# Attention scores, maxima and values by double steps, with TensorE's order as written

## The chip, the cores and the metric

The kernel runs on one core of a Trainium2 chip, in one launch. The core has five engines that this document names by the profile's short names: PE (TensorE, the matrix unit; PEld is its loading of weights), DVE (VectorE), ACT (ScalarE), POOL (GpSimd) and SP (SyncE, which issues the DMAs). Each runs its own list of instructions in order, and they wait for each other through semaphores. The metric is the time of one execution on the device in microseconds; the median of several executions is given.

## The reference, cut to what matters

Two layers on 512 latent tokens with a prefix of 256 context tokens, width 1024: an attention layer and a Mamba-2 layer, each followed by a gated feed-forward part. The change touches the attention layer alone:

```python
def gqa_attend(q, k, v):
    s = jnp.einsum('bqhgd,bkhd->bhgqk', q, k).astype(jnp.float32) * (HEAD_DIM ** -0.5)
    p = jax.nn.softmax(s, axis=-1).astype(v.dtype)
    return jnp.einsum('bhgqk,bkhd->bqhgd', p, v)

def attention_mixer(h_lat, h_ctx, w_qkv, q_norm, k_norm, w_o, need_ctx_out):
    q_l, k_l, v_l = jnp.split(h_lat @ w_qkv, [Q_DIM, Q_DIM + KV_DIM], axis=-1)
    ...
    k_all = jnp.concatenate([k_l, k_c], axis=1)
    v_all = jnp.concatenate([v_l, v_c], axis=1)
    ...
    o_l = ob.transpose(1, 0, 2, 3, 4, 5).reshape(bsz, seq, Q_DIM) @ w_o
    ...
        o_c = gqa_attend(q_c, k_c, v_c).reshape(bsz, l_ctx, Q_DIM) @ w_o
    return o_l, o_c
```

There are 16 query heads of 64 columns and 4 key heads. Latent queries attend to 768 keys, context queries to the 256 context keys. Queries and keys are normed and rotated first.

## The kernel before, in words

**Pairs and steps.** Heads are worked on two at a time: eight pairs (`Pair`), one head in partitions 0 to 63 and the other in 64 to 127. A pair has seven steps (`steps`, from L790). Steps 0 to 5 take one block of 128 keys each against all 512 latent queries; step 6 takes the two context blocks against the 256 context queries. A step is

- the **scores** (L835, L837): four pairs of matmuls into a PSUM tile `ps_s` of 1024 columns, three for the product in split precision and one that adds the negated row maxima (`diag`); 64 rows of the array for each head, so that the two run side by side ("64\*128" in the profile);
- the exponential (L838) on ACT into a tile `pr`, of which there are three;
- the sum over key blocks (L843, L845, L849) on DVE into `acc`.

What follows a step runs one step later (`later_lat`, `later_ctx`): the **values** (L799), matmuls of `pr` with the values of that key block into the PSUM bank `ps_o` or, for context, `ps_oc` ("128\*64"). After the last latent block and after the context blocks `final` closes the softmax: matmuls with ones over `acc` (L805, `ps_sum` or `ps_oc`), logarithm and exponential on ACT (L808, L809), three operations on DVE (L810 to L812).

**Maxima.** Row maxima of pair p + 1 are found while pair p runs (`maxima`, from L751): seven units, each of one or two scores in plain precision into a PSUM tile `ps_m` (L761, also "64\*128") and a reduction on DVE (L765). The last unit makes `diag` from them (L781, L786), so that the next pair's first scores need it.

**Buffers.** `ps_s` and `ps_m` share two PSUM tiles of two banks each (tag "S"). All else in PSUM shares four single banks (tag "B"): `ps_o`, `ps_sum`, `ps_oc`, the norms' `ssq`, and the filler's `ps_q`, `ps_ada`, `ps_adt`, `ps_d`.

**Filler.** Between steps a planner (`Weave`) puts other work on PE: projections of the later pairs' queries (`ps_q`), the modulation (`ps_ada`, `ps_adt`), and the output projection of finished pairs (`ps_d`), all but `ps_ada` with the whole array ("128\*128"). It divides what is left evenly over the 56 steps. "Lights" are small pieces with a due step and a condition, at most one a step: the chains that norm and rotate queries (`queries`, whose `ssq` matmuls are "64\*64"), splits of weights, splits of finished outputs (`osplit`). Lights that a pair's maxima need are run at the latest before these.

**The order on PE.** The loop (L965 to L992) emits, in each step: scores, a unit of maxima, the last step's values, filler. In the last step of a pair the maxima come before the scores. The framework's scheduler then orders the instructions of each engine. It follows the emitted order by priority, but moves instructions forward where its own model says that an earlier one isn't ready. An earlier part of attention, the first projections, pins PE, ACT and DVE to the emitted order (`manual_schedule`, L524 to L637); the steps don't.

**After the steps** the last pair's output is split (`osplit(7)`), and the projection of the last three pairs follows (`ps_dn`), then the feed-forward part.

Of the kernel before, what the change touches and what calls it, by code (L numbers as in the profile page):

```python
# [17 lines left out]
L = 512  # L18
# [3 lines left out]
NH = 16  # L22
# [489 lines left out]
def attention(g, adas, project, X):  # L512
# [4 lines left out]
    Bk, Sb = (lambda name: Bank(g, name)), (lambda name: S(g, name))  # L517
# [5 lines left out]
    ET = mybir.EngineType  # L523
# [220 lines left out]
    class Pair:  # L744
# [45 lines left out]
        def steps(self):  # L790

            (qh, ql), (kh, kl) = qprep[self.p], k2[self.kv]
            po = acc = None
            o = g.t3p.tile([P, T], F32, tag="o", bufs=2, name=f"o{self.p}")

            def values(po, pr, t, off, n, first, last):
                v = vt[t][:, self.kv * HD : (self.kv + 1) * HD]
                for e in range(2):
                    nc.tensor.matmul(po[S64[e], :n], v, pr[:, 512 * e + off : 512 * e + off + n], start=first, stop=last)  # L799

            def final(po, ps, acc, out):

                n = out.shape[-1]
                for e in range(2):
                    nc.tensor.matmul(ps[S64[e], :n], g.ones[:, :HD], acc[:, n * e : n * e + n], start=True, stop=True)  # L805
                y, u = t2("y")[:, :n], t2("u")[:, :n]

                nc.scalar.activation(y, ps, AF.Ln)  # L808
                nc.scalar.activation(y, y, AF.Exp, scale=-1.0)  # L809
                nc.vector.tensor_tensor(out, po, y, ALU.mult)  # L810
                nc.vector.scalar_tensor_tensor(u, ps, -1.0, y, ALU.mult, ALU.mult)
                nc.vector.scalar_tensor_tensor(out, u, 2.0, out, ALU.add, ALU.mult)  # L812

            def later_lat(po, pr, t, acc):
                values(po, pr, t, 0, L, t == 0, t == 5)
                if t == 5:
                    final(po, Bk("ps_sum"), acc, o[:, :L])

            def later_ctx(pr, acc):
                pc = Bk("ps_oc")  # L820
# [7 lines left out]
            for t in range(7):  # L828
                ps, pr = Sb("ps_s"), g.t3p.tile([P, 1024], F32, tag="pr", bufs=3, name="pr")
                for q0, n, k0, off in (((0, L, t * P, 0),) if t < 6 else ((L, C, L, 0), (L, C, L + P, C))):  # L830
                    q, k = slice(q0, q0 + n), slice(k0, k0 + P)
                    outs = [ps[:, 512 * e + off : 512 * e + off + n] for e in range(2)]
                    for i, (a, b) in enumerate(((kh, qh), (kl, qh), (kh, ql))):
                        for e in range(2):
                            nc.tensor.matmul(outs[e], a[S64[e], k], b[S64[e], q], start=i == 0, stop=False)  # L835
                    for e in range(2):
                        nc.tensor.matmul(outs[e], onesr[S64[e]], self.diag[S64[e], q], start=False, stop=True)  # L837
                nc.scalar.activation(pr, ps, AF.Exp)  # L838
                if t == 0:
                    po = Bk("ps_o")  # L840
                elif t == 1:
                    acc = g.t3p.tile([P, 1024], F32, tag="acc", bufs=1, name="acc")
                    nc.vector.tensor_tensor(acc, prev, pr, ALU.add)  # L843
                elif t < 6:
                    nc.vector.tensor_tensor(acc, acc, pr, ALU.add)  # L845
                else:
                    acc = t2("accc")
                    halves = pr.rearrange("p (e k q) -> p e k q", e=2, k=2)
                    nc.vector.tensor_tensor(acc.rearrange("p (e q) -> p e q", e=2), halves[:, :, 0], halves[:, :, 1], ALU.add)  # L849
                prev = pr  # L850
                yield (lambda t=t, pr=pr, po=po, acc=acc: later_lat(po, pr, t, acc)) if t < 6 else (
                    lambda pr=pr, acc=acc: later_ctx(pr, acc))
            g.o.append(o)

# [107 lines left out]
        pass  # L962
    for _ in qfirst:
        pass
    late_step = None  # L965
    for p in range(NH // 2):
        m = iter(())
        if p < 7:
            for it in [it for it in weave.lights if it in {2: q2, 3: q3}.get(p + 1, qc.get(p + 1, [])) + (kk if p == 3 else [])]:
                it.run()  # L970
                weave.lights.remove(it)
            m = pairs[p + 1].maxima()
        own = pairs[p].steps()
        for t in range(7):
            if t == 6:
                next(m, None)
            todo = next(own)
            if t < 6:
                next(m, None)
            if late_step:  # L980
                late_step()
            late_step = todo
            for it in list(free):
                if it.at <= weave.now and it.ready(weave.now):
                    it.run()
                    it.when = weave.now
                    free.remove(it)
            weave.step()
            if p == 7 and t == 3:
                osplit(6)  # L990
        next(own, None)
    late_step()  # L992
    assert not weave.lights, len(weave.lights)
    weave.drain()
    osplit(7)


# [722 lines left out]
```

## Time and profile before

| | us |
|---|---|
| median of 3 runs | 1887.12 (1885.73 to 1887.31) |
| span of the profiled execution | 1884.5 |
| first scores start | 111.14 |
| last projection (`ps_dn`) starts | 375.26 |
| busy from 111 to 376, of 265: PE, DVE, ACT | 259.61, 225.88, 130.11 |

The profiled execution has no time of its own beside its span; the span runs from the first to the last instruction of the program, and the median of the runs lies 2.6 us above it. In the profile's lines L835 is line 835 of the kernel; "out<-in" gives the tiles written and read; "64\*128 64x512" is the shape of the array that a matmul uses and its moving operand; "x8" counts instructions. A line of the timeline begins with the start and the duration in us, and "[0.60 <-DVE qsq]" is idle time of the engine before it and what ended it. A matmul's duration includes its way through the array, so that the next may start before it ends. A line of the waits gives the waiting engine, tile and line, whom it waited for, and in us the total, the number and the longest.

### The profile page before, as it was taken

To read this page: it belongs to the slowest core of one execution; us is meant where nothing else is said; L and a number is where in the kernel's file an instruction comes from. 1 tells how busy PE (TensorE), PEld (TensorE's weight loads), DVE (VectorE), ACT (ScalarE), POOL (GpSimd) and SP (SyncE) were. 2 spreads that over 40 slices of the span, in tenths; PEclk is the share of its full clock that TensorE was granted. 3 is DMA by queue.
4 is the path that set the end of the run, shared out by engine and by line. 5 is a ranking of instruction groups with operands and counts; after the bars stand their busy time and mean duration, and the time that the engine had idled before them with its cause. 6 is when DMAs were issued, how large, how long until landed. Compare 5 with 4: busy or idle time off the path is not lost.

```text
span 1884.5 us, 27447 instructions
## 1 busy us (share of the span) xinstructions
PE 1860.0 (99%) x10794; PEld 1531.3 (81%) x10794; DVE 1348.8 (72%) x2013; ACT 832.6 (44%) x1422; POOL 232.5 (12%) x220
## 2 busy tenths in 40 slices
PE   9999999999999999999999999999999999999999
PEld 7865545689888888888888888888887888888887
DVE  5688999678877777444478977777888676565655
ACT  3655544354222222222257577766667352323331
POOL 2100000030000000000031243443334200000000
PEclk9999999999999999999999999999999999999999
DMA  9223241015444554222224243434344323323332
GB/s 342 70 82 118 84 145 62 18 50 189 136 134 124 176 180 146 68 68 67 67 79 140 70 121 114 133 113 135 120 126 125 100 78 101 101 87 104 90 101 90
DMA packets 73489, 210.02 MB, mean 111 GB/s; under 512 B 8976, under 2 KB 14480, under 8 KB 73232
## 3 DMA queue, kind: packets, MB, share of 16 engines
q1 hardware_dynamic: 73360, 208.26, 35.2%
q8 instruction: 85, 1.39, 0.3%
q14 instruction: 44, 0.36, 0.1%
HBM read 198.79 MB, written 6.82 MB: 109 GB/s over the span
## 4 chain that ended last, share of the span: by engine, by line
PE 80%; DVE 10%; issue 4%; ACT 3%; DMA 2%; POOL 1%; SPq 0%; DVEq 0%; POOLq 0%; ACTq 0%
PE ps_up L105 10%; PE ps_up L106 10%; PE ps_up L108 10%; PE ps_d L105 6%; PE ps_d L108 6%; PE ps_d L106 5%; PE ps_in L105 4%; PE ps_in L108 4%; PE ps_in L106 3%; PE ps_o L799 2%; PE ps_s L835 2%; PE ps_st L1340 1%; DVE wl L87 1%; DVE xf L1212 1%; PE ps_wo L106 1%
## 5 line engine op out<-in xcount | busy, mean ns | idle before, releaser
L87 DVE TENSOR_TENSOR wl<-wst,wh 128x1024 fp32r<-128x1024 f32 x211 | 261.0, 1237 | 246.5 <-PE ps_up L106 125.4
L85 ACT CAST wh<-wst 128x1024 fp32r<-128x1024 f32 x211 | 220.8, 1048 | 413.5 <-DMA wst<-in_wup 316.2
L106 PE MATMUL ps_up<-hlf,wh 128*128 128x512 f32 x992 | 351.6, 354 | 0.0
L108 PE MATMUL ps_up<-hhf,wl 128*128 128x512 f32 x992 | 351.4, 354 | 0.0
L105 PE MATMUL ps_up<-hhf,wh 128*128 128x512 f32 x992 | 351.2, 355 | 0.0
L105 PEld LDWEIGHTS ps_up<-hhf,wh 128*128 128x128 f32 x992 | 187.5, 189 | 26.2
L106 PEld LDWEIGHTS ps_up<-hlf,wh 128*128 128x128 f32 x992 | 187.6, 189 | 26.0
L108 PEld LDWEIGHTS ps_up<-hhf,wl 128*128 128x128 f32 x992 | 187.5, 189 | 26.1
L105 PE MATMUL ps_in<-hhs,wh 128*128 128x512 f32 (+1 forms) x544 | 199.7, 367 | 0.0
L108 PE MATMUL ps_in<-hhs,wl 128*128 128x512 f32 (+1 forms) x544 | 193.5, 356 | 0.0
L106 PE MATMUL ps_in<-hls,wh 128*128 128x512 f32 (+1 forms) x544 | 193.3, 355 | 0.0
L108 PE MATMUL ps_d<-hdh,wl 128*128 128x512 f32 (+1 forms) x496 | 173.4, 350 | 0.0
L105 PE MATMUL ps_d<-hdh,wh 128*128 128x512 f32 (+1 forms) x496 | 173.3, 350 | 0.1
L106 PE MATMUL ps_d<-hdl,wh 128*128 128x512 f32 (+1 forms) x496 | 172.9, 349 | 0.0
L1022 DVE SCALAR_TENSOR_TENSOR X<-ps_d,mod,X 128x256 f32<-128x256 f32 (+1 forms) x176 | 102.7, 614 | 27.1 <-PE ps_d L108 27.0
L105 PEld LDWEIGHTS ps_in<-hhs,wh 128*128 128x128 f32 x544 | 102.8, 189 | 15.5 <-issue 1.9
L108 PEld LDWEIGHTS ps_in<-hhs,wl 128*128 128x128 f32 x544 | 102.7, 189 | 15.0
L106 PEld LDWEIGHTS ps_in<-hls,wh 128*128 128x128 f32 x544 | 102.9, 189 | 13.0
L106 PEld LDWEIGHTS ps_d<-hdl,wh 128*128 128x128 f32 x496 | 93.2, 188 | 14.4 <-DVE hdl L87 0.2
L108 PEld LDWEIGHTS ps_d<-hdh,wl 128*128 128x128 f32 x496 | 93.2, 188 | 13.1
L105 PEld LDWEIGHTS ps_d<-hdh,wh 128*128 128x128 f32 x496 | 93.0, 188 | 13.0 <-ACT hdh L85 0.3
L168 DVE SCALAR_TENSOR_TENSOR junk<-wada,cb 128x1024 f32<-128x1024 f32 x80 | 97.5, 1218 | 1.1 <-ACT cb L159 0.8
(375 smaller groups left out, 3632.9 us busy)
## 6 DMA issues: line engine op xcount, KB each, us to landing
wst<-in_wup SPq DMA_DIRECT2D x88, 512.0 KB, 3.5
wada<-in_adaT SPq DMA_DIRECT2D x56, 512.0 KB, 3.8
wst<-in_win SPq DMA_DIRECT2D x48, 512.0 KB, 3.6
wst<-in_wdown SPq DMA_DIRECT2D x44, 512.0 KB, 3.7
E<-ad SPq DMA_DIRECT2D x64, 256.0 KB, 6.7
wada<-in_adaB SPq DMA_DIRECT2D x24, 512.0 KB, 4.6
ec<-ead SPq DMA_DIRECT2D x64, 128.0 KB, 4.6
wst<-in_wout SPq DMA_DIRECT2D x16, 512.0 KB, 3.7
```

Source lines behind the costliest of these rows:

```text
L85: keep(nc.scalar.copy(hi, src))
L87: keep(eng.tensor_tensor(lo, src, _r(hi), ALU.subtract))
L105: mm(out, wh, ah, start=first, stop=False)
L106: mm(out, wh, al, start=False, stop=False)
L108: i = mm(out, wl, ah, start=False, stop=last)
L168: g.tc.keep_in_program_order(nc.vector.scalar_tensor_tensor(junk, w, 1.0, cb[:, v * D : (v + 1) * D], ALU.mult, ALU.mult, accum_out=md[:, ...
L799: nc.tensor.matmul(po[S64[e], :n], v, pr[:, 512 * e + off : 512 * e + off + n], start=first, stop=last)
L835: nc.tensor.matmul(outs[e], a[S64[e], k], b[S64[e], q], start=i == 0, stop=False)
L1022: nc.vector.scalar_tensor_tensor(ap, o[:, c0:c1], gate[:, m, v : v + 1], ap, ALU.mult, ALU.add)
L1212: i = nc.vector.scalar_tensor_tensor(cv, raw[:, tap : tap + n], par(f"sw{tap}", j), cv, ALU.mult, ALU.add)
L1340: nc.tensor.matmul(ps[:, d * 256 : (d + 1) * 256], Bt[:, t * P : (t + 1) * P], xw[d][t], start=t == ts[0], stop=t == ts[-1])
```

## The change

The loop takes the 56 steps two at a time, across the borders of pairs: 28 double steps. Each emits the scores of both steps, then the values (and closings) of the two steps before, then two units of maxima, then two portions of filler. The maxima of pairs 1 to 7 are one stream, drawn two units a double step after one unit ahead of the loop; the lights that a pair needs are run when the stream reaches it. PE keeps the emitted order over the whole loop and the drain of what is left (`manual_schedule` for PE); ACT, DVE and the rest stay with the scheduler. The bank `ps_o` is taken at the first values instead of the first scores. The split of pair 6's output is emitted before the late values of its double step. After the loop the last two steps' values and closings follow each other.

```diff
@@ steps @@
-            po = acc = None
+            po, acc = [], None
...
-            def later_lat(po, pr, t, acc):
-                values(po, pr, t, 0, L, t == 0, t == 5)
+            def later_lat(pr, t, acc):
+                if t == 0:
+                    po.append(Bk("ps_o"))
+                values(po[0], pr, t, 0, L, t == 0, t == 5)
                 if t == 5:
-                    final(po, Bk("ps_sum"), acc, o[:, :L])
+                    final(po[0], Bk("ps_sum"), acc, o[:, :L])
...
-                if t == 0:
-                    po = Bk("ps_o")
-                elif t == 1:
+                if t == 1:
...
@@ the loop @@
-    late_step = None
-    for p in range(NH // 2):
-        m = iter(())
-        if p < 7:
-            for it in [it for it in weave.lights if it in {2: q2, 3: q3}.get(p + 1, qc.get(p + 1, [])) + (kk if p == 3 else [])]:
+    def stream():
+
+        for p in range(1, NH // 2):
+            for it in [it for it in weave.lights if it in {2: q2, 3: q3}.get(p, qc.get(p, [])) + (kk if p == 4 else [])]:
                 it.run()
                 weave.lights.remove(it)
-            m = pairs[p + 1].maxima()
-        own = pairs[p].steps()
-        for t in range(7):
+            yield from pairs[p].maxima()
+
+    m, own, late = stream(), None, []
+    man = g.tc.manual_schedule(engines={ET.PE})
+    man.__enter__()
+    next(m)
+    for d in range(7 * NH // 4):
+        todo = []
+        for p, t in (divmod(2 * d, 7), divmod(2 * d + 1, 7)):
+            if t == 0:
+                own = pairs[p].steps()
+            todo.append(next(own))
             if t == 6:
-                next(m, None)
-            todo = next(own)
-            if t < 6:
-                next(m, None)
-            if late_step:
-                late_step()
-            late_step = todo
+                next(own, None)
+            if p == 7 and t == 4:
+                osplit(6)
+        for f in late:
+            f()
+        late = todo
+        for _ in range(2):
+            next(m, None)
+        for _ in range(2):
             for it in list(free):
                 if it.at <= weave.now and it.ready(weave.now):
                     it.run()
                     it.when = weave.now
                     free.remove(it)
             weave.step()
-            if p == 7 and t == 3:
-                osplit(6)
-        next(own, None)
-    late_step()
+    for f in late:
+        f()
     assert not weave.lights, len(weave.lights)
     weave.drain()
+    man.__exit__(None, None, None)
     osplit(7)
```

More of the change, by code (lines that the diff above doesn't have):

```diff
@@ L838, in steps @@
                 nc.scalar.activation(pr, ps, AF.Exp)
-                if t == 0:
-                    po = Bk("ps_o")
-                elif t == 1:
+                if t == 1:
                     acc = g.t3p.tile([P, 1024], F32, tag="acc", bufs=1, name="acc")
                     nc.vector.tensor_tensor(acc, prev, pr, ALU.add)
-                elif t < 6:
+                elif 0 < t < 6:
                     nc.vector.tensor_tensor(acc, acc, pr, ALU.add)
-                else:
+                elif t:
                     acc = t2("accc")
@@ L850, in steps @@
                 prev = pr
-                yield (lambda t=t, pr=pr, po=po, acc=acc: later_lat(po, pr, t, acc)) if t < 6 else (
+                yield (lambda t=t, pr=pr, acc=acc: later_lat(pr, t, acc)) if t < 6 else (
                     lambda pr=pr, acc=acc: later_ctx(pr, acc))
```

## The prediction

> **What bounds the kernel now.** The page comes first, for the engine that sets the end.
>
> ```profile
> span 1884.5 us, 27447 instructions
> PE 1860.0 (99%) x10794; PEld 1531.3 (81%) x10794; DVE 1348.8 (72%) x2013; ACT 832.6 (44%) x1422; POOL 232.5 (12%) x220
> PE 80%; DVE 10%; issue 4%; ACT 3%; DMA 2%; POOL 1%; SPq 0%; DVEq 0%; POOLq 0%; ACTq 0%
> ```
>
> The chain that ended last runs on PE for 80% of the span. A busy PE is not a PE at its peak, so I count from the starts of its matmuls. The change touches one stage only, from the first scores (111.1 us) to the output projection (375.3 us). Second view, the table of stretches: the stage, its middle, and the stretch in which DVE is fullest.
>
> ```profile
> 111.00:376.00 265.00, 259.61 (x1612) 148.43 (x1611) 225.88 (x324) 130.11 (x174) 0.00 (x0) 1.00 0.27 87
> 145.00:340.00 195.00, 190.53 (x1184) 107.69 (x1182) 175.54 (x249) 97.09 (x130) 0.00 (x0) 1.00 0.30 98
> 185.00:225.00 40.00, 37.45 (x241) 21.60 (x240) 36.78 (x50) 20.54 (x27) 0.00 (x0) 1.00 0.33 104
> ```
>
> After the stretch and its length stand PE, PE's weight loads, DVE and ACT. PE is nearly always in a matmul, but DVE is busy 175.54/195 = 0.90 of the middle and 36.78/40 = 0.92 of the fullest part. It is the second bound, close behind.
>
> Third view, PE alone in order of time: a single step, values with their closing sums, and a filler of nine matmuls.
>
> ```profile
> 185.84 0.49 PE L835 MATMUL ps_s<-qh,kh 64*128 64x512 f32 x2
> ...
> 186.63 0.39 PE L837 MATMUL ps_s<-diag,onesr 64*128 64x512 f32 x2
> 186.86 0.40 PE L761 MATMUL ps_m<-kh,qh 64*128 64x512 f32 x2
> 187.19 1.08 PE L799 MATMUL ps_o<-pr,v 128*64 128x512 f32 x4
> ...
> 173.00 1.08 PE L799 MATMUL ps_o<-pr,v 128*64 128x512 f32 x4
> 173.91 1.03 PE L805 MATMUL ps_sum<-acc,ones 128*64 128x512 f32 x4
> 174.87 0.64 PE L129 MATMUL ps_ada<-wada,sc 128*32 128x512 f32 x4
> ...
> 351.75 1.08 PE L799 MATMUL ps_o<-pr,v 128*64 128x512 f32 x4
> 352.76 0.50 PE L105 MATMUL ps_d<-hhol,wh 128*128 128x512 f32 x1
> ...
> 355.02 0.50 PE L835 MATMUL ps_s<-qh,kh 64*128 64x512 f32 x2
> ```
>
> Inside a run of one array shape (the pair of numbers behind the operands), pairs of score matmuls start 0.23 us apart (186.63 to 186.86). The run of four score pairs and a pair of maxima, all 64\*128, takes 187.19 - 185.84 = 1.35 us, though five times 0.23 is 1.15: **a run costs 0.20 us beyond its matmuls**. Values, 128\*64: alone 352.76 - 351.75 = 1.01; with as many closing matmuls 174.87 - 173.00 = 1.87; so four cost 0.86 and the run 0.15. Filler, 128\*128: nine take 355.02 - 352.76 = 2.26 against 9 x 0.23 = 2.07, so 0.2. A change of shape is what doubling steps saves.
>
> **The change part by part.** *Runs saved.* Two single steps are now six runs (scores with maxima, values, filler, twice): 2 x (0.20 + 0.15 + 0.20) = 1.10 us. A double step is four (scores, values, maxima, filler): 0.75. In the first 24 of 28 double steps that saves 0.35 each, 8.4 us. The last four have no maxima left and three runs: 0.55 saved each, 2.2 us. Against this stand fillers of another shape, which end a run of filler where before they were often the whole filler of a step:
>
> ```profile
> L129 PE MATMUL ps_ada<-wada,sc 128*32 128x512 f32 x96 | 11.5, 598 | 0.6 <-DVE qsq L690 0.6
> L677 PE MATMUL ssq<-qsq,ones 64*64 64x512 f32 (+1 forms) x56 | 10.6, 495 | 0.0
> ```
>
> At 16 and 8 instructions each these are 6 + 7 = 13 runs; at 0.2 they take back up to 2.6. Net 8.0.
>
> *Order as written.* Before, the scheduler may move PE's matmuls, and cuts score groups in two:
>
> ```profile
> 141.06 0.50 PE L835 MATMUL ps_s<-qh,kh 64*128 64x512 f32 x1
> 142.16 1.92 PE L129 MATMUL ps_ada<-wada,sc 128*32 128x512 f32 x16 [0.60 <-DVE qsq L690]
> ...
> 306.94 0.50 PE L835 MATMUL ps_s<-qh,kh 64*128 64x512 f32 x1
> 308.48 0.39 PE L105 MATMUL ps_d<-hhoc,wh 128*128 128x256 f32 x1 [1.04 <-DVE X L1022]
> ...
> PE ps_m L761 <- DVE ma L765: 3.3, 4, 1.2
> ACT pr L838 <- PE ps_s L837: 85.8, 38, 5.5
> ```
>
> Each cut adds two runs, 0.4 us; two cuts, 0.8 us back: **8.8 us saved in runs**. Waits of the old order: 142.16 - 141.06 - 0.23 = 0.9 and 308.48 - 306.94 - 0.23 = 1.3 in these cuts, and 3.3 in four waits of maxima for the last maxima's reduction: 5.5 us. The reductions are late because DVE is full, and DVE's work is not less; but a pair's last maxima now have a double step's filler ahead of the scores that need them. I take half, **2.7 us**, between nothing and 5.5.
>
> *New waits.* Work per operation is unchanged on ACT and DVE; rows:
>
> ```profile
> 187.06 1.02 ACT L838 ACTIVATE pr<-ps_s 128x1024 f32<-128x1024 f32 x1 [2.15 <-PE ps_s L837]
> ...
> L838 ACT ACTIVATE pr<-ps_s 128x1024 f32<-128x1024 f32 x56 | 57.1, 1021 | 85.9 <-PE ps_s L837 85.8
> L765 DVE TENSOR_REDUCE ma<-ps_m 128x2 f32<-128x1024 f32 (+1 forms) x35 | 42.8, 1222 | 5.8 <-PE ps_m L761 5.8
> L845 DVE TENSOR_TENSOR acc<-acc,pr 128x1024 f32<-128x1024 f32 x32 | 39.0, 1219 | 6.0 <-ACT pr L838 6.0
> L85 ACT CAST wh<-wst 128x1024 fp32r<-128x1024 f32 x10 | 10.4, 1045 | 8.4 <-DMA wst<-in_w_o 4.5 <-PE ps_ada L129 1.5 <-DVE wl L87 1.2
> ```
>
> Scores and maxima share two PSUM tiles ("S"). In a double step they go A, B for scores and A, B for maxima, so the second maxima wait for the second exponential, which itself needs one of three "pr" buffers: the one that the first values of this double step must have read. From the end of the second scores: values end at 0.15 + 0.86 = 1.0; the exponential starts at about 1.2 (187.06 is 0.2 us after the last score pair has streamed, 186.63 + 0.23) and ends at 2.2; PE arrives after both values and the first maxima, 0.15 + 2 x 0.86 + 0.33 = 2.2. It just fits if ACT is free. ACT does 130.11 - 57.1 = 73 us of other work in the stage, and only 38 of 56 exponentials found it idle, so I take 0.2 us on average, between 0 and one whole cast, 1.05. Where the late part holds closing sums (three of seven double steps) PE arrives 0.4 us or more later, so 14 of 24 count: **2.8 us** (0 to 14.7). Queued behind these maxima is all of PE, first the filler.
>
> The first maxima's reduction has the second maxima and the filler as cover, some 4 us; with two sums and two reductions at 1.22 DVE owes 4.9 of a double step of about 8.9 us. That hides it as long as DVE's other work keeps to the rest.
>
> Four other PSUM banks serve values, sums, context, norms and filler. Late parts of steps 5 and 6 now come at once in every second pair, and a norm holds two banks: the wait at 142.16 is such a case, 0.9 us. I take one more, **1.0** (0 to 4).
>
> *Start.*
>
> ```profile
> 111.14 0.50 PE L835 MATMUL ps_s<-qh,kh 64*128 64x512 f32 x2
> ...
> 112.40 0.50 PE L761 MATMUL ps_m<-kh,qh 64*128 64x256 f32 x4 [0.30 <-ACT qh L85]
> ...
> 113.15 1.51 PE L677 MATMUL ssq<-qsq,ones 64*64 64x512 f32 x8
> ...
> 113.26 1.22 DVE L765 TENSOR_REDUCE ma<-ps_m 128x4 f32<-128x1024 f32 x1
> ...
> 115.49 0.50 PE L835 MATMUL ps_s<-qh,kh 64*128 64x512 f32 x2
> ```
>
> The stream's first maxima now stand ahead of the first scores, and are ready at 112.40 only. Scores follow to 113.7; the second scores wait for the tile that the reduction frees at 113.26 + 1.22 = 114.5; with no values yet as cover, the second maxima wait for their exponential until 116.6. By then PE had before also done a norm and six filler matmuls, 115.49 - 113.15 = 2.34 us; less the extra maxima, **2.1 us lost** (1 to 3.5).
>
> *End.*
>
> ```profile
> 370.52 1.03 PE L805 MATMUL ps_sum<-acc,ones 128*64 128x512 f32 x4
> 373.81 1.08 PE L799 MATMUL ps_oc<-pr,v 128*64 128x256 f32 x8
> 375.26 0.39 PE L105 MATMUL ps_dn<-hhoc,wh 128*128 128x256 f32 x1
> 379.69 0.38 PE L105 MATMUL ps_dn<-hhoc,wh 128*128 128x256 f32 x1 [1.28 <-ACT wh L85]
> ```
>
> Before, filler stood between the last two closings. Now both come last, so that ACT's and DVE's closing work for 768 columns falls into the projection's start, which already waits 1.28 us. **1.0 us** (0 to 2).
>
> Sum: -8.8 - 2.7 + 2.8 + 1.0 + 2.1 + 1.0 = **-4.6 us**. The span 1884.5 would be 1879.9. The median shown is 1887.12, 2.6 above that span; I carry the difference unchanged: 1882.5 us. The weight DMAs and other stages keep their place behind PE and only shift.
>
> **The rivals.** *No new wait and all the old gone:* -8.8 - 5.5 + 2.1 = -12.2, so 1875. For it: old waits come from DVE's place in a step, and 8.8 is plain counting. Against: DVE at 0.90.
>
> *DVE becomes the bound:* if it can't do better than its present 0.90 in 145 to 340 us, that stretch keeps its 195 us, and three early and the last four double steps give 1.0 + 2.2, which start and end (3.1) take back: 1887. Against it: it reached 0.92 where PE pushed, and 0.92 would let the stretch shrink by 4 us, about what I forecast. [...] The starts of the matmuls, 0.23 us apart with the loads hidden, speak for PE.
>
> *Slower:* the second maxima find the exponential late every time. It has a 0.8 us hole ahead of it on ACT, which a scheduler fills; one cast there in each of 14 double steps costs 14 x 1.05 = 14.7 in place of 2.8, and the sum is +7.3: 1894. It decides from 0.2 + 4.6/14 = 0.53 us each. For it: 18 of 56 exponentials found ACT at work. Against: ACT is only half busy in this stage (130.11 of 265).
>
> *It does not do what it says:* order as written could still be cut by other shapes; that is in the 2.6.
>
> **How the numbers follow.** Forecast (1879 to 1886) 0.50; all waits gone 0.20; DVE 0.12; slower 0.18. A measurement of this kernel can tell about 0.2%, 3.8 us, from no change. The forecast lies just past it: 0.32 of its 0.50 I count as faster, 0.18 as same. Faster 0.52, same 0.30, slower 0.18. The range takes in the favourable case to 1874 and the slower one to 1892, leaving out its end and some of what I don't see.
>
> **What would show it.** Runs of PE in the stage: some 60 fewer changes of shape, with 0.2 us each still (if fewer, the first step fails). The last projection would start near 370.7 in place of 375.26. Waits of maxima for the exponential, absent before, would be some 3 us; if 10 or more, the slower rival. DVE's share in the middle should rise to about 0.92; if it stays 0.90 with PE waiting for reductions, DVE is the bound. The first norm should start near 117 in place of 113.15. Wrong altogether would be a longer stage without such waits, or a difference outside it.

## The result and the profile after

The changed kernel takes 1904.68 us (median of 4 runs, 1901.75 to 1905.77); the kernel before took 1887.21 beside it. The medians differ by 17.5 us. The ratio on record is 1.0084, with a 95% interval of 1.0072 to 1.0096, which is 15.9 us: **slower by 16 to 17.5 us**, where I had forecast 4.6 faster, and outside the range. The profiled execution took 1905.67 us.

First the page of the changed kernel: span, busy time by engine, the chain that ended last.

```profile
span 1903.8 us, 27448 instructions
PE 1859.9 (98%) x10794; PEld 1540.1 (81%) x10794; DVE 1347.7 (71%) x2013; ACT 833.0 (44%) x1422; POOL 231.2 (12%) x220
PE 82%; DVE 10%; ACT 3%; issue 2%; DMA 2%; POOL 0%; DVEq 0%; SPq 0%; ACTq 0%; POOLq 0%
```

PE is busy as long as before (1860.0) in a span that is 19.3 us longer. The work is the same, and by the page what was added is idle time of PE. (Its busy time hides two changes that nearly cancel, which the account below takes apart.) The table of stretches of the changed kernel shows where (columns: stretch, its length, PE, PE's weight loads, DVE, ACT, POOL, granted clock, DMA share, GB/s):

```profile
111.00:392.00 281.00, 258.87 (x1607) 156.90 (x1608) 224.54 (x321) 130.26 (x173) 0.00 (x0) 0.96 0.25 83
145.00:340.00 195.00, 176.94 (x1101) 105.06 (x1101) 163.31 (x236) 92.46 (x124) 0.00 (x0) 0.95 0.29 96
185.00:225.00 40.00, 35.64 (x210) 20.38 (x204) 30.79 (x41) 21.97 (x29) 0.00 (x0) 0.91 0.31 102
```

In the middle, PE's busy time fell from 190.53 to 176.94 of 195 us and DVE's from 175.54 to 163.31: nothing is fuller than before. New is the clock: 0.95 in the middle and 0.91 in the third row, where before had 1.00 throughout. Third, the start and the two ends in the timeline of PE:

```profile
112.07 0.51 PE L761 MATMUL ps_m<-kh,qh 64*128 64x256 f32 x4 [1.19 <-ACT qh L85]
...
114.20 0.50 PE L837 MATMUL ps_s<-qh,kh 64*128 64x512 f32 x2 [0.69 <-DVE ma L765]
...
117.01 1.51 PE L677 MATMUL ssq<-qsq,ones 64*64 64x512 f32 x8
...
391.58 0.38 PE L105 MATMUL ps_dn<-hhoc,wh 128*128 128x256 f32 x1
...
395.53 0.36 PE L105 MATMUL ps_dn<-hhoc,wh 128*128 128x256 f32 x1 [1.40 <-DVE u L811]
```

The last projection starts at 391.58 in place of 375.26: 16.3 of the span's 19.3 us arise in the attention stage. Fourth, what PE waited for in this stage (111 to 392 us; in all, times, longest):

```profile
PE ps_m L761 <- ACT pr L840: 6.2, 7, 2.7
PE ps_adt L135 <- DVE qsq L690: 3.2, 1, 3.2
PE ps_m L761 <- ACT qh L85: 2.9, 2, 1.7
PE ps_d L105 <- DVE X L1031: 2.2, 2, 1.6
PE ps_d L105 <- DVE u L811: 2.1, 1, 2.1
PE ps_s L837 <- DVE ma L765: 2.0, 3, 0.7
PE ps_s L837 <- DVE mb L765: 1.2, 1, 1.2
PE ssq L677 <- DVE o L810: 0.7, 1, 0.7
PE ps_q L105 <- DVE o L810: 0.6, 1, 0.6
PE ssq L677 <- ACT qsq L668: 0.5, 1, 0.5
PE ps_q L105 <- ACT qs L735: 0.5, 1, 0.5
```

The rows add up to 22.1 us. The same view of the kernel before, from 111 to 376 us, has four rows and 5.2 us, the 3.3 us that the prediction shows and these:

```profile
PE ps_d L105 <- DVE X L1022: 1.0, 1, 1.0
PE ps_ada L129 <- DVE qsq L690: 0.6, 1, 0.6
PE ps_m L761 <- ACT qh L85: 0.3, 1, 0.3
```

So 16.9 us of waits were added, of many kinds, none of them above 6.2 us.

**The half clock.** All rows are of one profiled execution, and executions of one kernel differ: over a whole execution the kernel before had a mean granted clock of 0.997 to 1.000. The records of the granted clock show it at one half four times in the stage, for 3.41, 3.41, 3.41 and 10.24 us, 20.5 us in all; before has none there. The four starts, at 163.15, 190.46, 210.94 and 316.75 us, are 27.31, 20.48 and 105.81 us apart, 8, 6 and 31 times 3.413: they lie on one grid of 3.413 us. The stretches ahead of the four and the slow ones, in the table of stretches of the changed kernel (the second column of busy time less the length gives PE's idle time, the number after POOL is the clock):

```profile
159.74:163.15 3.41, 1.33 (x12) 1.27 (x14) 1.25 (x4) 1.27 (x2) 0.00 (x0) 1.00 0.36 88
163.15:166.56 3.41, 3.41 (x18) 2.29 (x16) 2.10 (x3) 1.02 (x1) 0.00 (x0) 0.50 0.00 0
187.05:190.46 3.41, 1.76 (x10) 0.54 (x10) 3.24 (x4) 3.19 (x7) 0.00 (x0) 1.00 0.29 67
207.53:210.94 3.41, 0.70 (x6) 0.30 (x5) 3.37 (x4) 3.35 (x5) 0.00 (x0) 1.00 0.00 0
313.34:316.75 3.41, 1.70 (x16) 1.36 (x15) 3.41 (x6) 0.88 (x2) 0.00 (x0) 1.00 0.00 0
316.75:327.00 10.25, 8.66 (x40) 7.25 (x39) 5.60 (x14) 1.02 (x1) 0.00 (x0) 0.50 0.00 0
```

Ahead of each slow stretch PE was idle for about half a grid stretch or more: 3.41 - 1.33 = 2.08, 1.65, 2.71 and 1.71 us. The price is read from equal matmuls of the filler in the timeline of the changed kernel, ahead of the fall and behind it:

```profile
315.98 0.28 PE L106 MATMUL ps_d<-hloc,wh 128*128 128x256 f32 x1
...
316.57 0.28 PE L105 MATMUL ps_d<-hhoc,wh 128*128 128x256 f32 x1
...
317.07 0.42 PE L105 MATMUL ps_d<-hhoc,wh 128*128 128x256 f32 x1
...
318.77 0.42 PE L108 MATMUL ps_d<-hhoc,wl 128*128 128x256 f32 x1
```

Five intervals take 0.59 us, 0.118 each; then eight take 1.70, 0.213 each. Of PE's time at half clock 1 - 0.118/0.213 = 0.45 is lost. PE was busy all through the three short slow stretches and for 8.66 us of the long one, 3 x 3.41 + 8.66 = 18.9 us, so some **8.4 us**, an estimate from this one place.

**The account.** Counted from the starts of PE's matmuls, the stage had 181 runs of one array shape before and has 121 now. At the prices of the prediction (0.15 to 0.20 us) a run costs 0.18 on average: 32.4 us before, 22.0 now, so the runs **save 10.4 us**. The matmuls themselves, by their spacing inside such runs, are 221.1 us in both. -10.4 + 16.9 + 8.4 = +14.9 of the 16.3 us. The other 1.4 us stay open. They lie within PE's busy time, so that the prices of a run and of the half clock, both read from a few places, are the first suspects. The remaining 3 us of the span lie behind the stage, some 0.7 of them in the projection's start.

### The profile page after: what moved, and what is told of

Read it like the earlier page. It is cut to its first block, busy times and chain, and to the rows that moved or that the text cites. A ratio compares the mean times of both kernels' runs of the same rounds, so it can differ in the third digit from the quotient of the medians.

```text
span 1903.8 us, 27448 instructions
## 1 busy us (share of the span) xinstructions
PE 1859.9 (98%) x10794; PEld 1540.1 (81%) x10794; DVE 1347.7 (71%) x2013; ACT 833.0 (44%) x1422; POOL 231.2 (12%) x220
## 4 chain that ended last, share of the span: by engine, by line
PE 82%; DVE 10%; ACT 3%; issue 2%; DMA 2%; POOL 0%; DVEq 0%; SPq 0%; ACTq 0%; POOLq 0%
PE ps_up L105 10%; PE ps_up L106 10%; PE ps_up L108 10%; PE ps_d L105 6%; PE ps_d L108 5%; PE ps_d L106 5%; PE ps_in L105 4%; PE ps_in L108 4%; PE ps_in L106 4%; PE ps_s L837 2%; PE ps_st L1349 2%; PE ps_o L799 1%; PE ps_wo L106 1%; PE ps_wo L108 1%; PE ps_wo L105 1%
## 5 line engine op out<-in xcount | busy, mean ns | idle before, releaser
L105 PEld LDWEIGHTS ps_up<-hhf,wh 128*128 128x128 f32 x992 | 187.6, 189 | 26.1
```

Of the source, the lines that this page charges most:

```text
L105: mm(out, wh, ah, start=first, stop=False)
```

## The experiments

Two theories stood at the outset. In the texts on record "theory A" is the first of them, with the taker that an experiment aims at named in each. *Fixed order:* PE in its written order has to stand behind each matmul that is not ready, where the scheduler would have moved another forward; the double steps ask for more at once, and the waits bring the half clock. *One taker:* a single resource is under it: the exponential's place on ACT, the three `pr` buffers, the four banks, the order of the maxima, or DVE's share. The table holds all runs; "runs" are runs of one shape, "waits" the sum of the rows of the view of PE's waits, "half clock" the time at it, all between 111 us and the start of the last projection.

| kernel | median us | ratio to before (95%) | runs | waits us | half clock us | projection starts |
|---|---|---|---|---|---|---|
| before | 1887.21 | | 181 | 5.2 | 0 | 375.3 |
| after | 1904.68 | 1.0084 (1.0072 to 1.0096) | 121 | 22.1 | 20.5 | 391.6 |
| e1_free_order | 1894.33 | 1.0027 (1.0016 to 1.0037) | 152 | 8.3 | 3.4 | 380.9 |
| e2_single_kept | 1893.90 | 1.0030 (1.0020 to 1.0040) | 172 | 11.5 | 3.4 | 382.0 |
| e9_last_pair | 1887.16 | 0.9996 (0.9986 to 1.0005) | 173 | 5.7 | 3.4 | 377.1 |
| e3_pr4 | 1927.22 | 1.0207 (1.0176 to 1.0238) | 121 | 21.4 | 30.7 | 394.0 |
| e5_m_between | 1909.09 | 1.0108 (1.0088 to 1.0128) | 135 | 26.1 | 17.1 | 397.1 |
| e6_act_behind | 1904.57 | 1.0090 (1.0073 to 1.0106) | 121 | 23.4 | 20.5 | 392.4 |
| e7_adt_later | 1912.85 | 1.0129 (1.0114 to 1.0144) | 117 | 27.8 | 13.7 | 396.3 |
| e8_both_q7 | 1913.12 | 1.0133 (1.0118 to 1.0148) | 117 | 28.9 | 20.5 | 401.3 |
| e10_exp_first | 1903.37 | 1.0074 (1.0059 to 1.0089) | 121 | 21.9 | 17.1 | 393.3 |
| e11_banks | 1905.60 | 1.0084 (1.0069 to 1.0099) | 121 | 23.7 | 23.9 | 394.0 |
| e12_all | 1910.79 | 1.0112 (1.0096 to 1.0129) | 121 | 27.9 | 17.1 | 394.4 |
| e14_few_sums | 1901.36 | 1.0072 (1.0058 to 1.0085) | 121 | 21.3 | 13.7 | 388.2 |
| e15_before_few | 1883.88 | 0.9977 (0.9967 to 0.9987) | 177 | 5.0 | 0 | 372.5 |
| e17_free_all | 1908.51 | 1.0102 (1.0082 to 1.0122) | 145 | 18.4 | 34.1 | 398.0 |
| e13_single | 1885.89 | 0.9983 (0.9973 to 0.9993) | 175 | 6.0 | 3.4 | 374.4 |
| e16_last_single | 1884.61 | 0.9978 (0.9970 to 0.9987) | 167 | 5.9 | 6.8 | 372.4 |

The kernel before beside the later runs took 1888.3 to 1889.5 us. Each ratio is to the runs of before beside it, so kernels are compared by the ratios. Waits, half clock and the rest are of one profiled execution of each kernel; a difference of 1 us between two of them proves little.

### The two halves of the change

*e1_free_order* is the changed kernel with PE's order left to the scheduler:

```diff
-    man = g.tc.manual_schedule(engines={ET.PE})
-    man.__enter__()
...
-    man.__exit__(None, None, None)
```

> The changed kernel with PE's order left to the scheduler again, all else as changed. Theory A (the time goes into waits of PE in the kept order: second maxima for the exponential, norms and filler for a bank, and the slow clock that long waits bring): other matmuls move into the waits, so no slow clock in the stage and a projection that starts near 375 to 380 us instead of 391.6; 1887 to 1893 us in all. Rival B (double steps cost the time wherever PE's order comes from, through DVE and the buffers): within 4 us of the changed kernel, 1901 to 1906.

*e2_single_kept* is the kernel before, single steps and all, with those three lines added around its loop:

> The kernel before, single steps, with PE's order kept as written over the same stretch; nothing else changed. If keeping the order is what costs, whatever the steps (rival C): 10 us or more above before, 1897 to 1905. If it needs the double steps (theory A: maxima follow an exponential that starts late): within 5 us of before, 1884 to 1892, changes of shape about 170 (181 before).

Measured: each half alone is about 0.3% slower than before, both together 0.84%. The first lies just above theory A's range and far below the rival's; the second lies between its two ranges, so the fixed order costs something with single steps too. Two rows of PE's waits in e1_free_order:

```profile
PE ps_m L761 <- ACT pr L840: 2.0, 3, 1.3
PE ps_adt L135 <- DVE qsq L690: 1.4, 1, 1.4
```

and the largest one in e2_single_kept:

```profile
PE ps_m L761 <- DVE ma L765: 4.3, 5, 1.3
```

With the same double steps, freeing the order takes waits from 22.1 to 8.3 and half clock from 20.5 to 3.4 us, and gives 31 of the 60 saved runs back. With single steps, keeping the order more than doubles the waits, 5.2 to 11.5; the longest single one there, 3.20 us, of the modulation's transposes (`ps_adt`) for a bank that a norm holds, is the very one of the changed kernel. Beyond streaming and runs the stage held 10.7 us before, 19.1 with the order alone, 20.9 with double steps alone, 37.3 with both: the halves add 8.4 and 10.2 and together 26.6, 8 more than their sum. The small parts of the change (where `ps_o` is taken, the unit of maxima ahead of the loop, the place of pair 6's split) stay in e1_free_order and count here with the double steps.

*e9_last_pair* has double steps in the last pair alone, where no maxima are left, and the order free:

```diff
-            if late_step:
+            if p < 7 or t == 0:
+                if late_step:
+                    late_step()
+                late_step = todo
+            elif t % 2:
+                held.append(todo)
+                continue
+            else:
...
+                for f in held[:-1]:
+                    f()
+                held, late_step = held[-1:] + [todo], lambda: None
...
```

> The kernel before, order free, with double steps in the last pair alone (scores of steps 1 and 2, 3 and 4, 5 and 6 together, values and filler likewise), where there are no maxima and DVE has room. Counted in runs it saves 3 x 0.55 = 1.6 us; no new wait is expected but up to 1 us at the end, where the last closings fall together: 1885 to 1888, 0 to 2 us under before; the stage's first 340 us unchanged. If double steps cost waits even without maxima: 1889 or more.

Measured: no difference that can be told (0.9996). Eight runs fewer are worth some 1.4 us, below what the measurement resolves.

### One taker at a time

*e3_pr4* gives a fourth `pr` buffer; to make room, the tiles of 1024 columns that hold weights among other things are 9 instead of 10:

```diff
-                ps, pr = Sb("ps_s"), g.t3p.tile([P, 1024], F32, tag="pr", bufs=3, name="pr")
+                ps, pr = Sb("ps_s"), g.t3p.tile([P, 1024], F32, tag="pr", bufs=4, name="pr")
...
-    return g.p.tile([P, 1024], dt, tag="t4", bufs=10, name=name)
+    return g.p.tile([P, 1024], dt, tag="t4", bufs=9, name=name)
```

> The changed kernel with four pr buffers instead of three; to make room the weight tiles (tag t4) have nine instead of ten. The second exponential need no longer wait for the first values, so there is no hole of 0.8 us ahead of it. Theory A with the buffer as its main part: the waits of maxima for the exponential (13.9 us of PE's weight loads, 6.2 of its matmuls) fall to a third, the episodes of slow clock at 190 and 211 us go, the projection starts 6 to 10 us earlier than 391.6. If ACT's own order is the cause and the hole only the occasion: waits fall by less than a third. If banks and DVE are the main part (rival): projection within 3 us of 391.6. Outside the stage the missing weight tile may cost some us, so the stage is compared.

Measured: the waits for the exponential fell from 6.2 to 4.0 us, but the longest, 2.7 us, stayed; the sum of waits hardly fell (21.4 for 22.1). Of the 23 us that it is slower than the changed kernel, 19.5 lie behind the start of the last projection. The missing weight tile may be why, which was not looked into; the time as a whole does not speak on `pr`, the stage does.

*e5_m_between* puts the two maxima between the two portions of filler, to give the exponential more time:

```diff
-        for _ in range(2):
-            next(m, None)
-        for _ in range(2):
+        for i in range(2):
...
+            if i == 0:
+                next(m, None)
+                next(m, None)
```

> The changed kernel with the two units of maxima between the two portions of filler instead of ahead of them: one more change of shape in each of 24 double steps, 24 x 0.2 = 4.8 us more in runs. Theory A: the wait for the exponential goes nearly (2 us of filler stand ahead), but the reductions have half the cover ahead of the next scores; waits of scores for reductions rise from 3 to 5 to 10 us; in sum 1893 to 1902. If the wait for the exponential costs little: 1905 to 1912.

Two rows of PE's waits:

```profile
PE ps_s L837 <- DVE ma L765: 7.6, 9, 1.5
PE ps_s L839 <- DVE diag L786: 6.6, 5, 2.1
```

The waits for the exponential are gone from the view; the reductions and the `diag` made from them are late instead, since less filler stands between the maxima and the scores that need their tile. The same few microseconds of cover can stand ahead of the maxima or behind them, not both.

*The place on ACT.* The longest wait for the exponential in the changed kernel, from its timeline:

```profile
204.55 1.03 ACT L840 ACTIVATE pr<-ps_s 128x1024 f32<-128x1024 f32 x1 [2.80 <-PE ps_s L839]
...
206.20 0.84 ACT L703 CAST kh<-raw 64x768 fp32r<-64x768 f32 x1 [0.62 <-DVE raw L692]
...
208.76 0.83 ACT L704 CAST kh<-raw 64x768 fp32r<-64x768 f32 x1
209.50 1.01 ACT L840 ACTIVATE pr<-ps_s 128x1024 f32<-128x1024 f32 x1
...
210.56 0.51 PE L761 MATMUL ps_m<-kh,qh 64*128 64x256 f32 x4 [2.71 <-ACT pr L840]
```

ACT is idle for 0.62 us ahead of 206.20, until the input of a cast is there. Four casts of the keys, 3.3 us, come from there on, and the exponential, the maxima and all of PE stand behind them. The prediction had the missing `pr` buffer as the reason for the hole. It is not needed for it: with the fourth buffer of e3_pr4 the same four casts come first, and PE waits as long:

```profile
210.27 0.50 PE L761 MATMUL ps_m<-kh,qh 64*128 64x256 f32 x4 [2.69 <-ACT pr L840]
```

So what makes this wait is the order of ACT's list. *e6_act_behind* orders the casts and the norm's scaling behind the latest exponential issued:

```diff
-            nc.scalar.copy(h[s], qs[s])
+            ordered(g, nc.scalar.copy(h[s], qs[s]), g.exp[0])
...
-                nc.scalar.activation(pr, ps, AF.Exp)
+                g.exp[0] = nc.scalar.activation(pr, ps, AF.Exp)
```

> The changed kernel, where ACT's casts of keys (L703, L704) and its gain in a query's norm (L669) are ordered behind the latest double step's second exponential; before, the scheduler put them into the hole ahead of it (four casts of 0.83 us at 206 to 209.6 us). If ACT's order is what makes the second maxima late (theory A): PE's matmul waits of maxima for the exponential fall from 6.2 to under 2.5 us, the slow clock at 211 us goes, projection at 384 to 389 instead of 391.6, 1897 to 1902. If the hole itself (the pr buffers) is: less than 1 us changes.

Measured: 1904.57, as the changed kernel. The casts stand in the same place (a 2.70 us wait is left), because when they are emitted the latest exponential is the one ahead of the hole. So this run does not test ACT's order. *e10_exp_first* does: it gives the exponential priority in the scheduler.

```diff
-                nc.scalar.activation(pr, ps, AF.Exp)
+                with g.tc.high_priority():
+                    nc.scalar.activation(pr, ps, AF.Exp)
```

> The changed kernel with one edit: the exponentials have the scheduler's highest priority on ACT, so that of two operations that are ready the exponential is first. If older work of ACT in the hole ahead of the second exponential makes the second maxima late (theory A): the wait at 207.9 us falls from 2.7 to about 1 us, PE's matmul waits of maxima for the exponential from 6.2 to 2 to 4, and the slow clock at 211 us goes; projection 3 to 6 us earlier than 391.6. If the hole alone does it (pr buffers): waits within 1.5 us of 6.2.

From its timeline, the same place:

```profile
208.97 1.02 ACT L841 ACTIVATE pr<-ps_s 128x1024 f32<-128x1024 f32 x1
...
210.04 0.50 PE L761 MATMUL ps_m<-kh,qh 64*128 64x256 f32 x4 [1.14 <-ACT pr L841]
```

Two of the casts now come behind the exponential, the wait fell from 2.71 to 1.14 us, and the half clock at 211 us is gone. All waits for the exponential fell from 6.2 to 4.6 us. Yet the sum of waits is 21.9 (22.1), half clock came at 262 and 272 us in its place, the projection starts later (393.3 for 391.6, where 3 to 6 us earlier was expected), and the time is 1903.37.

*The banks.* *e7_adt_later* lets the modulation's units rest for four steps instead of two, so that the transposes at 158 us no longer meet a norm:

```diff
-                    j.cool = self.now + 2
+                    j.cool = self.now + 4
```

> The changed kernel, where the modulation's second half (adt) comes four planner steps after its first half instead of two, so that it no longer stands on PE right behind a norm that holds two banks (PE waited 3.2 us there, at 158.6). If the kept order meets a full set of banks there (theory A): that wait goes, the slow clock at 163 us goes, projection 4 to 6 us earlier than 391.6, 1899 to 1902. If the wait only moves to the next taker of a bank (rival): a wait of 1.5 us or more at the same norm, and less than 2 us gained.

Measured: that wait and the half clock behind it are gone, and the modulation, now shifted, waits for its weights:

```profile
PE ps_ada L129 <- DMA wada<-in_adaB: 6.8, 3, 3.7
```

*e8_both_q7* has both edits (e6, e7) and makes the chain for pair 7's queries due at step 34 instead of 36:

> Both edits together, and the norm of pair 7's queries due two steps earlier (34 instead of 36), since PE waited 1.7 us for that pair's queries at 313.6 us, with 10.2 us of slow clock behind it. If waits and the slow clock behind them are all of the loss (theory A): at most one slow episode, rest beyond streaming and runs near 20 us instead of 37, projection at 374 to 380, 1884 to 1893. If DVE bounds the stage (rival): new waits for DVE in their place, projection later than 384, 1895 or more.

Measured: the waits for queries fell from 2.9 to 1.2 us; the weights' DMA (9.3) and the banks of `ps_d` (5.2) took their place, 1913.12 us. *e11_banks* frees the norm's banks early in another way: ACT copies the sums of squares out of PSUM, and the norm works on the copy, with DVE taking over one operation of ACT's (0.95 us more for DVE in each norm):

```diff
+        for ps, c in ss:
+            nc.scalar.copy(sq[:, c], ps)
...
-        nc.scalar.activation(u, y, AF.Square)
-        for ps, c in ss:
-            nc.vector.scalar_tensor_tensor(u[:, c], ps, HD * EPS, u[:, c], ALU.add, ALU.mult)
+        nc.vector.scalar_tensor_tensor(u, sq, HD * EPS, y, ALU.add, ALU.mult)
+        nc.vector.tensor_tensor(u, u, y, ALU.mult)
```

> The changed kernel with one edit: a norm's sums (ssq) are copied by ACT out of their two PSUM banks at once, and the rest of the norm works on the copy; the banks come free after two ACT operations instead of after four and one of DVE. DVE's work is the same count of operations plus one of 0.95 us in each norm, ACT's about 0.1 us more. Theory A (the kept order meets a full set of banks): the 3.2 us wait at 158.6 falls to 1 us or less and no slow clock follows at 163; waits at the other norms (188.6, 223.5, 305.4 us) shrink; projection 4 to 8 us earlier. If DVE's share is the bound (rival): waits come back as waits for DVE, projection within 2 us of 391.6.

From its timeline:

```profile
162.37 1.05 PE L135 MATMUL ps_adt<-cst,ada_sb 128*128 128x2 f32 x8 [0.25 <-ACT qsq L680]
...
318.79 0.94 DVE L692 SCALAR_TENSOR_TENSOR qs<-qsq,qs 128x768 f32<-128x768 f32 x1
...
320.65 0.79 PE L761 MATMUL ps_m<-kh,qh 64*128 64x256 f32 x4 [4.86 <-ACT qh L85]
```

The edit did its part: 3.19 us became 0.25. But pair 7's norm ends later on DVE, and the maxima that need its queries wait 4.86 us in place of 1.71. *e12_all* has the edits of e10 and e11, the reductions at high priority as well, and the start as before (no unit of maxima ahead of the loop, three in the first double step):

> Both edits, reductions of maxima with the highest priority on DVE as well, and the stream's first unit of maxima no longer ahead of the first scores (three units in the first double step). Theory A (waits for the exponential, for banks, for reductions, the start, and the slow clock behind long waits are all of the loss): rest beyond streaming and runs falls from 37 to 12 to 20 us, at most one slow episode, projection at 366 to 376, 1877 to 1889. If DVE bounds the stage: rest over 25, projection later than 380, 1892 or more.

Measured: 1910.79. Its waits are 27.9 us, led by 5.6 for queries and 5.4 for `diag`. This is what its text expects if DVE bounds the stage, which the next section tests directly. In all eight runs that touch one taker or several, the sum of waits stayed between 21.4 and 28.9 us. None of the takers tried is under the others.

### DVE's share

What could still be under all of them is DVE. *e14_few_sums* leaves out the running sum's additions at t = 2, 3 and 4 of each pair (the first addition starts from one more), so that it does less than the reference asks; *e15_before_few* is the kernel before with the same left out:

```diff
-                    nc.vector.tensor_tensor(acc, prev, pr, ALU.add)
-                elif 0 < t < 6:
+                    nc.vector.scalar_tensor_tensor(acc, prev, 1.0, pr, ALU.add, ALU.add)
+                elif t == 5:
                     nc.vector.tensor_tensor(acc, acc, pr, ALU.add)
...
```

> The changed kernel with three of the five additions to the running sum of the exponentials left out for every pair (t = 2, 3, 4; the first addition starts from one more, so that the sum stays above zero): 24 additions of 1.22 us, so 29 us less VectorE work in the stage, and the sums are not those of the reference. If VectorE's share is what the waits follow (reductions, norm's products and table corrections late, queries late behind them), the stage's waits and half clock of 37 us beyond streaming and run cost fall to below 20 us and the time to some 1885. If the waits come from the fixed order on TensorE meeting ScalarE's order, four PSUM banks and three pr buffers, they stay at 30 us or more and the time stays within 6 us of 1905, as in all the runs that took one taker away.

> The same 24 additions left out of the kernel before: the control. Its waits beyond streaming and run cost are 10.7 us. If VectorE's share set them, they fall to some 5 us and the time to 1881; if not, the time stays within 3 us of 1887.

The table of stretches and two waits of e14_few_sums:

```profile
145.00:340.00 195.00, 177.68 (x1117) 103.85 (x1116) 148.15 (x223) 94.81 (x128) 0.00 (x0) 0.96 0.30 99
```

```profile
PE ps_m L761 <- ACT pr L840: 7.6, 8, 2.1
PE ps_adt L135 <- DVE qsq L690: 3.2, 1, 3.2
```

DVE's share of the middle falls from 163.31/195 = 0.84 to 0.76, and the waits from 22.1 to 21.3; beyond streaming and runs the stage keeps 33.9 of 37.3 us. The control holds 8.6 in place of 10.7, with waits of 5.0 for 5.2, and is 0.23% faster than before: DVE's work is worth something there, between the two cases of its text. In the changed kernel the ratio, 1.0072, is at the edge of the interval of 1.0072 to 1.0096, so no gain can be told. **DVE's share is not what the waits follow**; the waits for banks and for the exponential are there with DVE at 0.76.

### Free order, and the better version

*e17_free_all* joins e1's free order with the three edits (exponential and reductions at high priority, norm's banks):

> The changed kernel without the kept order and with the same three edits. With TensorE's order left to the scheduler the double steps had 20.9 us beyond streaming and run cost in the stage, and 1894.3 us. If ScalarE's order and the banks made those waits, they halve and the time falls to some 1886; if double steps meet waits by their own size (two scores ask for two exponentials, two reductions and the filler at once), the time stays within 3 us of 1894.

Neither came: 1908.51, 14 us above e1. The largest of its waits:

```profile
PE ps_m L761 <- ACT qh L85: 6.8, 2, 3.9
```

and the clock was at half for 34.1 us, 13.7 of them at once from 113 us on. The edits that moved waits under the fixed order do so under the free one too. *e13_single* puts the same three edits into the kernel before, and *e16_last_single* into e9:

> The kernel before, single steps and free order, with the same three edits to ACT's and DVE's order and to the norms' banks. It tells what these edits do without double steps: theory A expects little, as before had few such waits (3.3 us of maxima for reductions, 0.9 for a bank): 1883 to 1888. If the edits help alike in both orders, what e12 gains is not evidence on double steps: 1880 or less.

> The kernel before with the double steps in the last pair alone and with the three edits of the single-step run (exponential and reductions at high priority, norm's squares copied out of PSUM at once). If the parts add, -1.5 us each from the run count of the last pair and -2 us from the edits: 1884. If the double steps bring waits even in the last pair, it is no faster than the single-step run's 1885.9.

Measured: 0.9983 and 0.9978 of before. Both are some 0.2% faster than before, about what can be told, though their waits are not fewer (6.0 and 5.9 for 5.2); their intervals overlap, so whether the last pair's doubling adds to the edits stays open.

## Why the prediction was wrong

**What held.** Runs: 60 fewer changes of shape, as said, worth 10.4 us at the prices read. (I had 8.8: of the 13 runs that I set against 64 saved ones, only 4 came.) Start: the norm comes at 117.01, as said; 1.19 + 0.69 + 0.28 + 0.42 us of waits there against 0.30 before are 2.3, for 2.1. The old waits went, all 4.9 us but the start's; I had taken half.

**The step that failed is "New waits".** The waits for the exponential were sized at half of what came (+2.8 for +5.5 us), those for PSUM banks at a ninth (+1.0 for +9.3), those for reductions and for queries at nothing (for +2.5 and +1.7), and that waits bring the half clock was not considered (+8.4). By the rows of the waits after, sorted by what PE waited for:

| term of the sum | predicted us | measured us |
|---|---|---|
| runs | -8.8 | -10.4 |
| old waits | -2.7 | -4.9 |
| second maxima for the exponential | +2.8 | +5.5 (6.2 less the start's 0.7) |
| PSUM banks (`qsq`, `X`, `u`, `o`, `qs` L735) | +1.0 (0 to 4) | +9.3 |
| scores for reductions | 0, "hides it" | +2.5 (3.2 less the start's 0.7) |
| maxima for pair 7's queries | 0 | +1.7 (2.9 less the start's 1.2) |
| start | +2.1 | +2.3 |
| half clock | not considered | +8.4 |

With 0.5 for a norm's squares and the 1.4 that stay open these make the stage's +16.3. The end, predicted at +1.0, lies behind it and was near: the projection's first waits are 1.40 us and less, for 1.28 before, some 0.7 us more in all.

*Banks*, the worst: I took one more wait like that at 142.16, "0.9 us". That one is short in the fixed order too: at the same `ps_ada` in e2_single_kept PE stands idle for 1.08 us. The longest wait, 3.2 us, is one that the trace of before does not show at all. There the modulation's transposes come long behind the norm, and without a wait:

```profile
156.49 1.51 PE L677 MATMUL ssq<-qsq,ones 64*64 64x512 f32 x8
...
163.34 1.05 PE L135 MATMUL ps_adt<-cst,ada_sb 128*128 128x2 f32 x8
```

Between the two the scheduler had put the scores and maxima of two steps, values and filler. In e2_single_kept, steps single and PE's order as written, the transposes are the next thing behind the norm:

```profile
158.16 1.51 PE L677 MATMUL ssq<-qsq,ones 64*64 64x512 f32 x8
162.87 1.05 PE L135 MATMUL ps_adt<-cst,ada_sb 128*128 128x2 f32 x8 [3.20 <-DVE qsq L690]
```

A trace of a free order shows only the waits that are left after the scheduler's moves, and is no list of those that a fixed order will meet. That is the error of the argument: I counted the loss of the free order only as two cuts and a few waits *saved*.

*The exponential*: the average of 0.2 us was too small. There were few late cases (7, two of them at the start, of 24 double steps), but with up to four casts ahead of the exponential, not one, and a free `pr` does not take the longest away (e3_pr4). The slower rival (late every time, 1894) is not what happened: 6.2 us, not the "10 or more" set for it. It had the sign, by another mechanism.

*DVE as the bound* (1887) is refuted by its share in the middle, 0.84 where 0.90 to 0.92 was expected, and by e14_few_sums. The changed kernel lost 16 us in this stage while DVE's busy time stayed (225.88 and 224.54), so the loss does not show in DVE's occupancy.

*The clock* I left out, as before showed 1.00. It is a second price on waits: the 16.9 us of added waits cost some 8.4 more.

**What is shown and what is not.** Shown: the fixed order and the double steps each add waits, and together more than their sum; a wait that an edit aims at goes or shrinks (e7, e10, e11), but the sum of waits does not fall; DVE's share is not under it. Argued only: that it is the order of the greedy lists on ACT and DVE, which each edit reshuffles, that puts the next wait in place. Open: the 1.4 us within PE's busy time, which of e17's three edits costs 14 us, and whether an order written out for ACT and DVE as well would let the 10.4 us through; neither was tried.

## What to carry to other kernels

A wait seen under a free order is what the scheduler left over, and the waits that it removed altogether leave no row; before fixing an engine's order, count each matmul that it had moved past a waiting one as a wait of its full length (here one of 3.20 us stood in no row of before). Work in larger portions saves the fixed cost per portion (here 0.15 to 0.20 us a run, 10.4 us in all), but asks for buffers, exponentials and reductions in bursts, and the cover for one of them is taken from the next. If removing a wait leaves the sum of waits where it was, measure the halves of the change apart before touching a further taker.

## What the hardware showed that was not expected

In these traces the clock falls to one half for whole stretches of a grid of 3.413 us (3.41 us three times and 10.24 us once in the changed kernel), and waits shorter than one stretch were enough. In the changed kernel three falls follow single waits of 3.19, 2.71 and 1.71 us, and the one at 190.46 us follows two, of 1.00 and 0.66 us, in one stretch. I put this grid under the traces of 16 kernels (all but before and e15_before_few, which have no slow stretch in the stage to place it by), and counted the full-speed stretches that touch 105 to 400 us by PE's idle time in them (3.413 us less its busy time), and how many were followed by a slow one:

| PE idle in a stretch of 3.41 us | stretches | next at half clock |
|---|---|---|
| under 0.7 us | 1145 | 2 |
| 0.7 to 1.0 | 45 | 2 |
| 1.0 to 1.4 | 63 | 5 |
| 1.4 to 1.7 | 27 | 8 |
| 1.7 to 2.0 | 22 | 17 |
| over 2.0 | 26 | 26 |

The changed kernel alone has 82 of these stretches, by row 69, 3, 4, 2, 2 and 2, of which 0, 0, 0, 1, 1 and 2 were followed by a slow one.

So in these kernels half clock goes with the sum of the idle time within a stretch, with the turn at about half of it: 8 of 27 stretches with 1.4 to 1.7 us idle were followed by it and 17 of 22 with 1.7 to 2.0. Two stretches with less than 0.7 us idle were followed by it all the same, and why is open. Where a wait falls on the grid mostly decides whether it costs a further 3.41 x 0.45 = 1.5 us (an estimate from the spacing above): in the changed kernel the wait of 2.12 us that ends at 335.57 us is parted by the grid, 1.75 us of it in the later stretch, and no slow one follows, while 1.71 us, all in one stretch, were followed by 10.24 us at half clock.
